# A hybrid decoder block on one core: dilated values formed for two slots at a time

## The chip, the cores and the metric

The kernel runs on one core of a Trainium2 chip. The metric is the device time of one execution in microseconds (us); lower is better. The kernel before takes 1284.16 us, the median of three runs (1284.13 to 1284.34).

The engines are called PE (TensorE, matrix products), DVE (VectorE), ACT (ScalarE), POOL (GpSimd) and SP (SyncE, which here only issues transfers). PE reads its operands from on-chip memory and adds its products up in banks of 512 float columns, which DVE and ACT read. Each engine works through its own instructions in the order in which the program wrote them; an instruction that waits for another engine holds up everything behind it on its own engine.

## The reference, cut to what matters

```python
h = h + 0.5 * swiglu(rms_norm(h, g_ffn1), w_ffn1_gate, w_ffn1_up, w_ffn1_down)
u = rms_norm(h, g_mix)
z = u @ w_in
a_glu, q, k, v, gate_logits = jnp.split(z, split_pts, axis=-1)
y_conv = conformer_conv(a_glu, w_dw, b_dw, g_conv_ln, b_conv_ln, w_conv_out)
q, k = rotary(q, cos, sin), rotary(k, cos, sin)
for gi, (window, dilation) in enumerate(((128, 1), (512, 4), (2048, 16))):
    hs = slice(gi * 4, (gi + 1) * 4)
    o_g, lse_g = dilated_window_attention(q[:, :, hs], k[:, :, hs], v[:, :, hs],
                                          dilation, window // dilation)
alpha = softmax(stack(lses), axis=0)
y_attn = sum(alpha * outs) @ w_attn_out
h = h + (sigmoid(g_a) * y_conv + sigmoid(g_b) * y_attn) @ w_mix_out
h = h + 0.5 * swiglu(rms_norm(h, g_ffn2), ...)
h = h + sigmoid(rms_norm(h, g_ple) @ w_ple_gate) * (p @ w_ple_proj)
return rms_norm(h, g_final)
```

512 positions, width 1024, 12 heads of 128 in three groups of four. The four heads of a group are the four "slots": slot s is head s of each group.

## The kernel before, in words

**Operands.** Every float operand is cut into a high and a low part (`split`, L466: ACT casts the high part, DVE subtracts the rest), and every product is three: high times high, high times low, low times high (`mm3`, L453). Weights come in slabs of 128 x 1024 in the order that `slab_order` (L134) lists. `slab(key)` (L436) is called when a slab is used, and at that moment it starts the work on later ones: loads up to `AHEAD + RAW` slabs ahead, sums of weights up to `AHEAD + SUMS` ahead (`sum_one`, L296; L317, L321, L325 and L340 on DVE), and their splits `AHEAD` = 2 slabs ahead (`split_one`, L392; L402 on ACT, L403 on DVE). For slabs of the kinds "win", "v", "v0", "ao" and "co" the low part is formed by a transfer: ACT writes the negated high part (L372), and POOL issues a transfer that adds the weight to it (L374), four slabs ahead. The slab buffers come from a pool of 16.

**A unit** (`unit`, L458) is 24 products of 512 columns, eight blocks of 128 rows times three, summed in one bank. Its argument `beside` maps a block number to a function that is called ahead of that block and so puts other products among the unit's own.

**The loop over slots** (L1371 to L1431) runs four times. Each time it forms, in this order:

- the value of the first group (slab "v0"): one unit, then L1378; it is transposed later by `turn0`, ahead of block 6 of the next unit;
- three times a query and a key: six units, each followed by `rotary` (L1178; L1180, L1181, L1182, L1188, L1190, L1195, then L1200 or L1203);
- the values of the two dilated groups (slab "v", two per slot): for each of 8 blocks of rows, 4 classes of positions and 3 products, one product of 256 columns, into two banks; then four casts (L1424) and four subtractions (L1427).

**Attention** (class at L1216) of a slot is spread over the next slot's units. `last` forms the scores of the dilated groups ahead of blocks 4 and 6 of the next slot's first unit (L1248 reads them); `step(n)` is called after unit n: n = 0 starts `soft`, the exponentials (L1264) and an exchange of statistics through DRAM (SP, L1160 and L1164 into the tile `other`); n = 4 and 5 transpose the weights (`turn`, L1311, L1316, L1317); n = 5 and 6 multiply them with the values (`values`, banks `po`). `fill(n)` is called from `rotary`: n = 2 reads `other` (`weigh(0)`, L1282 to L1285), n = 3 computes the factors and scales the weights (L1287 to L1296). The unit with n = 4 carries the slot's own scores of the first group and starts their exponentials. Functions put on the list `soon` are taken by `some(n)`, two and four at a time in `rotary` and six after the first unit of a slot. Functions on the list `between` run in the next `rotary`.

**Background.** The depthwise convolution is a list `bg` of DVE instructions (31 taps per tile, L1087 and L1094, closed by L1099 and L1112). `background(n)` takes the next n: 4 after the first unit of a slot, 3 in each `rotary`, 1 after each block of the dilated values and 1 more in each half of their evacuation. After the slots come 16 gate units (L1485 to L1502), each with `side(6)`: six items of `bg`, or, once `bg` is empty, one step of `lns`. `lns` (L1469) is the layer norm of the convolution in 19 steps; a gate unit takes one more of them ahead of its block 4 (`half`). Its `root` forms the sums on PE (`ss`), its `spread` the row R, `normal` scales (L1445), `swish` applies silu (L1449) and splits (L471 and L472) two tiles each. Eight half units `ao` (L1506) take one step each; what is left runs ahead of the `co` units.

**The `co` units and the mixing.** Eight units `co` (L1521) multiply the normed convolution (`cvh`, `cvl`) with their weights. After each, up to `N_FORM` = 10 jobs of the list `later` run, then L1527 and L1528 form the gated sum, then new jobs are listed by `form_pair` (L630; L639 and L654 on DVE, L651 on ACT). After the last unit `N_FIRST` = 7 jobs run. Then the mixing product (L1540) goes through seven quarter products in the order B11, T1, T2, B22, T3, B21, T4 (`quarters_of`, L702); B11 and T2 share the bank `pa`, and after each one `add` (L713; L726) adds the bank to the residual `h`.

Of the kernel before, what the change touches and what calls it, by code (L numbers as in the profile page):

```python
# [10 lines left out]
F32 = mybir.dt.float32  # L11
# [7 lines left out]
P = 128  # L19
# [56 lines left out]
        ("dn", 2, 0), ("dn", 2, 1), ("gu", 9), ("gu", 10), ("dp", 0), ("dn", 3, 0), ("dn", 3, 1))  # L76
BY_ = False
N_FORM = 10
N_FIRST = 7
AFTER_M = {"B11": 0, "T1": 3, "T2": 3, "B22": 2, "T3": 2, "B21": 2, "T4": 2}  # L80
AFTER = {"B11": 1, "B21": 1, "T2": 1, "T1": 1, "T3": 2, "B22": 2}
# [52 lines left out]
def slab_order():  # L134
    out = []
    out += ffn_order("1")
    for c in range(KD):
        out += [("win", 8 + c), ("win", c)]
    for s in range(NSLOT):
        out += [("v0", s)]  # L140
        for g in range(NG):
            out += [("win", 16 + 4 * g + s), ("win", 28 + 4 * g + s)]
        out += [("v", s, j) for j in range(2)]
    out += [("win", 48 + m) for m in range(KD)]
    out += [("win", 40 + m) for m in range(KD)]
    out += [("ao", j) for j in range(4)]
    out += [("co", m) for m in range(KD)]
    out += [("m", ("mx", g), q) for g in range(2) for q in MIXED]
    out += ffn_order("2")
    out += [("pT",), ("pp", 0), ("pp", 1)]  # L150
    out += [("pg", m) for m in range(KD)]
    return out
# [3 lines left out]
def block_kernel(ctx: ExitStack, tc: tile.TileContext, a, out):  # L156
# [17 lines left out]
    def T(n, dt=F32, w=S):  # L174
        return act.tile([P, w], dt, name=name(n), tag="t", bufs=NT)
# [11 lines left out]
    def by_block(t):  # L187

        return t.rearrange("p (c b i) -> p b c i", c=NB, b=NB)

    def blocks(t):

        return t.rearrange("p (b c i) -> p b c i", c=NB, b=NB)

    def bank(n="ps", tag="ps"):
        return psum.tile([P, S], F32, name=name(n), tag=tag, bufs=6 if tag == "ps" else 2)
# [31 lines left out]
    def sources(key):  # L228

        if key[0] == "v0":  # L230
            return [(slice(2 * j, 2 * j + 2), slice(0, HD), blocks_of(a["w_v"][key[1], j], 2)[:, :, :HD])
                    for j in range(4)]
        if key[0] == "v":
            return [(slice(2 * i, 2 * i + 2), slice(0, 2 * HD), blocks_of(a["w_v"][key[1], 2 * key[2] + i], 2)[:, :, HD:])
                    for i in range(2)]
        if key[0] == "gq":
            return row_of(quarter(key[1], ("gu", key[2]), key[3]))
        if key[0] == "dp":
            at, k = (2 * P * z for z in ROUNDS[key[2]])
            return row_of([a["w_ffn%s_down" % key[1]][key[3] + i][:, at:at + k] for i in range(2)])  # L240
        src = source(key)
        if len(src.shape) == 3:
            return [(slice(0, KD), slice(0, P), src)]
        return [(None, slice(0, src.shape[-1]), src)]

    def blocks_of(t, k):
        return t.rearrange("p (k c) -> p k c", k=k)
# [11 lines left out]
    def product(key):  # L259
        return key[2] if key[0] in ("1", "2", "m") else None  # L260
# [162 lines left out]
    def ahead(what, one, to):  # L423
        while state[what] < min(to, len(order)):
            one()
# [10 lines left out]
    def slab(key):  # L436
        i = state["use"]
        assert order[i] == key, (order[i], key)
        state["use"] = i + 1
        more, sums = (1, 1) if key[0] == "gq" else (MORE, SUMS)  # L440
        for j in range(i + 1, i + AHEAD + sums + 1):
            ahead("load", load_one, j + 1)
            ahead("sum", sum_one, j + 1)
            soon_(i, j)
            ahead("split", split_one, min(j, i + AHEAD) + 1)
        if state["early"] < len(order) and product(order[state["early"]]) == "T4":
            soon_(i, i + LEAD["T4"])
        ahead("load", load_one, i + AHEAD + RAW + 1)
        if product(order[min(i + AHEAD + RAW, len(order) - 1)]):
            ahead("load", load_one, i + AHEAD + RAW + more + 1)  # L450
        return halves.pop(i)

    def mm3(ps, wh, wl, xh, xl, start, stop, part=False):  # L453
# [4 lines left out]
    def unit(ps, key, xs, ks=range(KD), beside={}):  # L458
        h, l = slab(key)
        for k in ks:  # L460
            if k in beside:
                beside[k]()
            c = slice(k * P, (k + 1) * P)
            mm3(ps, h[:, c], l[:, c], xs[k][0], xs[k][1], k == ks[0], k == ks[-1])

# [902 lines left out]

            return {2: (nothing, lambda: self.weigh(0)), 3: (scale, nothing)}.get(n, (nothing,) * 2)

    before = None  # L1371
    for s in range(NSLOT):
        q, k = [], []
        now = Attention(q, k)
        p = bank("pq")
        unit(p, ("v0", s), us, beside=before.last() if before else {})
        v0 = T("v0")
        V.tensor_mul(blocks(v0), by_block(p), by_block(R))  # L1378
        p = None
        if before is not None:  # L1380
            before.step(0)
        some(6)
        background(N_V0)

        def turn0():
            p = bank("pt")
            for b in range(NB):
                PE.transpose(p[:, b * P:(b + 1) * P], v0[:, b * P:(b + 1) * P], ident)
            now.v0 = split(p, "v")

        n = 1
        for g in range(NG):
            for base, dst in ((16, q), (28, k)):
                p = bank("pq")
                unit(p, ("win", base + 4 * g + s), us,
                     beside=now.scores(range(NB)) if n == 4 else {N_TURN: turn0} if n == 1 else {})
                if before is not None:
                    before.step(n)
                if n == 4:
                    now.soft(range(NB))  # L1400
                dst.append(rotary(p, "qk", N_QK[n - 1], g == 0, g > 0 and base == 16, *([before.fill(n)] if before else [])))
                p = None
                n += 1
        v0 = None
        q = k = None
        pv = [bank("pv") for _ in range(2)]
        for j in range(2):
            wh, wl = (blocks_of(z, 4) for z in slab(("v", s, j)))
            for kk in range(4):
                for c in range(NB):  # L1410
                    xh, xl = (classes(z)[:, c] for z in us[4 * j + kk])
                    po, at = pv[c // 2][:, c % 2 * 2 * P:(c % 2 + 1) * 2 * P], 4 * j + kk
                    PE.matmul(po, xh, wh[:, kk], start=at == 0 and c % 2 == 0, stop=False, skip_group_check=True)
                    PE.matmul(po, xh, wl[:, kk], start=False, stop=False, skip_group_check=True)
                    PE.matmul(po, xl, wh[:, kk], start=False, stop=at == KD - 1, skip_group_check=True)
                background(N_V)
        wh = wl = None
        now.v = []
        for c in range(NB):
            now.v.append(T("v12", F32R))  # L1420
        zs = [pv[c // 2][:, c % 2 * 2 * P:(c % 2 + 1) * 2 * P] for c in range(NB)]
        for cs in ((0, 2), (1, 3)):
            for c in cs:
                A.activation(now.v[c][:, :2 * P], zs[c], AF.Copy, scale=rcls[:, c:c + 1])  # L1424
            background(1)
            for c in cs:
                V.scalar_tensor_tensor(now.v[c][:, 2 * P:], zs[c], rcls[:, c:c + 1], now.v[c][:, :2 * P].bitcast(F32),  # L1427
                                       op0=OP.mult, op1=OP.subtract)
        now.v = [(t[:, :2 * P], t[:, 2 * P:]) for t in now.v]
        pv = zs = None  # L1430
        before, now = now, None  # L1431


# [52 lines left out]
    for base in (48, 40):  # L1486
        for m in range(KD):
            p = bank("pg")
            unit(p, ("win", base + m), us, beside={4: half} if n else before.last())
            t = T("sg")  # L1490
            V.tensor_mul(t, p, R)
            A.activation(t, t, AF.Sigmoid)
            sg[base, m] = t
            if n < 10:
                before.step(n, 2)
                some(6)
                for f in before.fill(n - 1):
                    f()
                while between:
                    between.pop(0)()  # L1500
            n += 1
            side(N_GATE)  # L1502
    before = None
    us.clear()
    background(len(bg))
    for j in range(4):  # L1506
# [14 lines left out]
    for m in range(KD):  # L1521
        p = bank("py")
        unit(p, ("co", m), cv)
        for _ in range(min(N_FORM, len(later))):
            next_job(later)
        t = sg[40, m]
        V.tensor_mul(t, t, p)  # L1527
        V.tensor_add(t, t, sg.pop((48, m)))  # L1528
        if m < 4:
            begun.append(form_pair(t, None, mixes[m], by=BY))  # L1530
        else:
            form_pair(sg.pop((40, m - 4)), sg.pop((40, m)), mixes[m - 4], None, begun[m - 4], BY)
# [205 lines left out]
```

## Time and profile before

| | us |
|---|---|
| median of three runs | 1284.16 |
| the profiled execution, its own time | 1284.48 |
| its span in the profile | 1282.6 |
| slots 0 to 3 (first "v0" unit to the last value product) | about 437 to 666.5 |
| gate units | 666.5 to 764.0 |
| `ao`, `co`, start of the mixing | 764.0, 786.3, 829.8 |

A row of a timeline gives the start of an instruction from the start of the span, its duration, engine, line, operation, what it writes and reads, and in brackets the engine's idle time before it and what ended it. A merged row (x4) gives the whole stretch. A row of windows gives the stretch, then for each engine asked for its busy time and count, then the granted clock, the share of the transfer engines and GB/s. A row of waits names who waited for whom: total, times, longest. Matmul durations overlap; what counts is the time from one start to the next.

### The profile page before, as it was taken

Reading aid. Unit: us, or ns where it says so; the run is one execution under the profiler, and the core shown is the slowest. Engines: PE = TensorE matmul, PEld = TensorE weight load, DVE = VectorE, ACT = ScalarE, POOL = GpSimd, SP = SyncE. Lnnn points to the kernel's source line nnn. Section 1 sums busy time; section 2 is a strip of 40 time slices with the busy share of each in tenths; the row PEclk is TensorE's granted clock in tenths of the full one; section 3 lists DMA queues with packets and bytes.
Section 4 is the critical chain, followed back from the end, with each engine's and each line's share of the span. In section 5 each row is a group of like instructions: output and inputs, shape, how many; then the busy total and the mean of one; then the engine's idle time right before and its main releaser. Section 6 shows DMA issues by size and latency. Waiting matters only on the chain.

```text
span 1282.6 us, 21795 instructions
## 1 busy us (share of the span) xinstructions
PE 1268.7 (99%) x8266; PEld 1163.1 (91%) x8266; DVE 1015.2 (79%) x1617; ACT 741.4 (58%) x1088; POOL 300.6 (23%) x392
## 2 busy tenths in 40 slices
PE   9999999999999999999999999999999999999997
PEld 7899999998988888989898888898899999998986
DVE  6988778898969887878778756786988888785865
ACT  6667566575633264746555445363777566585652
POOL 3122132132223232323332222012122122132000
PEclk9999999999999999999999999999999999999999
DMA  9676886867879889897887779567576876868641
GB/s 295 155 171 160 199 208 152 207 166 191 193 180 231 208 154 202 152 191 150 172 184 169 167 186 224 144 134 206 132 188 152 203 205 147 211 157 198 145 106 59
DMA packets 118224, 226.12 MB, mean 176 GB/s; under 512 B 20584, under 2 KB 54760, under 8 KB 118120
## 3 DMA queue, kind: packets, MB, share of 16 engines
q0 software_dynamic: 49600, 142.10, 54.3%
q1 hardware_dynamic: 68232, 82.37, 20.5%
q8 instruction: 65, 1.06, 0.3%
q14 instruction: 39, 0.32, 0.1%
q10 hardware_dynamic: 288, 0.26, 0.1%
HBM read 168.56 MB, written 2.13 MB: 133 GB/s over the span
## 4 chain that ended last, share of the span: by engine, by line
PE 74%; DVE 3%; DMA 1%; issue 1%; ACT 0%; SPq 0%; DVEq 0%
PE pa L708 5%; PE pa L709 5%; PE pa L711 5%; PE pq L454 4%; PE pq L455 4%; PE pq L456 4%; PE pg L454 3%; PE pg L456 3%; PE pg L455 3%; PE pd L711 2%; PE pd L709 2%; PE pd L708 2%; PE pb L455 2%; PE pb L454 2%; PE pb L456 2%; PE pe L711 1%
## 5 line engine op out<-in xcount | busy, mean ns | idle before, releaser
L374 POOL DMA_DIRECT2D wl<-wr x108 | 93.4, 867 | 439.8 <-ACT wl L372 341.1
L708 PE MATMUL pa<-bh,wh 128*128 128x256 f32 x680 | 167.5, 283 | 0.5 <-DVE gx L723 0.4
L709 PE MATMUL pa<-bl,wh 128*128 128x256 f32 x680 | 167.2, 283 | 0.0
L1094 DVE SCALAR_TENSOR_TENSOR acc<-glu,taps,acc 128x511 f32<-128x511 f32 (+14 forms) x240 | 161.6, 733 | 0.0
L403 DVE TENSOR_TENSOR wl<-s,wh 128x1024 fp32r<-128x1024 f32 (+1 forms) x96 | 108.5, 1132 | 38.1 <-ACT wh L402 37.8
L372 ACT ACTIVATE wl<-wh 128x1024 fp32r<-128x1024 f32 x84 | 87.9, 1051 | 80.3 <-DMA wh<-in_w_in 54.8
L708 PEld LDWEIGHTS pa<-bh,wh 128*128 128x128 f32 x680 | 130.5, 192 | 1.0 <-issue 0.5
L709 PEld LDWEIGHTS pa<-bl,wh 128*128 128x128 f32 x680 | 130.5, 192 | 0.0
L372 ACT ACTIVATE wl<-wr 128x1024 fp32r<-128x1024 f32 (+1 forms) x108 | 105.8, 980 | 26.0 <-DVE wl L403 11.5
L402 ACT ACTIVATE wh<-s 128x1024 fp32r<-128x1024 f32 (+1 forms) x96 | 92.9, 969 | 35.0 <-PE pd L455 13.4
L386 ACT ACTIVATE wh<-wr 128x1024 fp32r<-128x1024 f32 (+1 forms) x108 | 105.5, 977 | 12.0 <-PE pd L711 6.1
L708 PE MATMUL pd<-bh,wh 128*128 128x256 f32 x448 | 110.3, 283 | 0.0
L709 PE MATMUL pd<-bl,wh 128*128 128x256 f32 x448 | 110.2, 283 | 0.0
L374 POOL DMA_DIRECT2D wl<-in_w_in x56 | 48.5, 869 | 219.7 <-ACT wl L372 200.6
L711 PE MATMUL pa<-bh,wl 128*128 128x256 f32 x680 | 96.9, 283 | 0.0
L454 PE MATMUL pq<-xsh,wh 128*128 128x512 f32 x224 | 88.7, 396 | 0.0
L711 PEld LDWEIGHTS pa<-bh,wl 128*128 128x128 f32 x680 | 88.4, 192 | 0.0
L455 PE MATMUL pq<-xsl,wh 128*128 128x512 f32 x224 | 87.3, 390 | 0.0
L456 PE MATMUL pq<-xsh,wl 128*128 128x512 f32 x224 | 87.3, 390 | 0.0
L708 PEld LDWEIGHTS pd<-bh,wh 128*128 128x128 f32 x448 | 86.0, 192 | 0.0
L709 PEld LDWEIGHTS pd<-bl,wh 128*128 128x128 f32 x448 | 86.0, 192 | 0.0
L454 PE MATMUL pg<-xsh,wh 128*128 128x512 f32 x192 | 76.2, 397 | 0.3 <-ACT xsh L474 0.3
(330 smaller groups left out, 3615.4 us busy)
## 6 DMA issues: line engine op xcount, KB each, us to landing
wl<-wr POOLq DMA_DIRECT2D x72, 512.0 KB, 5.6
wh<-in_w_in POOLq DMA_DIRECT2D x56, 512.0 KB, 7.2
wl<-in_w_in POOLq DMA_DIRECT2D x56, 512.0 KB, 6.0
wr<-in_w_ffn_up SPq DMA_DIRECT2D x80, 256.0 KB, 4.3
wr<-in_w_ffn_gate SPq DMA_DIRECT2D x78, 256.0 KB, 4.7
wr<-in_w_ffn_down SPq DMA_DIRECT2D x96, 192.0 KB, 3.8
wl<-wr POOLq DMA_DIRECT2D x36, 384.0 KB, 4.4
wr<-in_w_ffn_down SPq DMA_DIRECT2D x16, 256.0 KB, 4.5
```

The lines of the kernel that those rows point to most:

```text
L372: A.activation(l.bitcast(F32R), h, AF.Copy, scale=-1.0)
L374: G.dma_start(to, src, accum_op=OP.add)
L386: A.activation(h, r, AF.Copy)
L402: A.activation(h, r, AF.Copy)
L403: V.tensor_sub(l, r, h.bitcast(F32))
L454: PE.matmul(ps, wh, xh, start=start, stop=False, skip_group_check=part)
L455: PE.matmul(ps, wh, xl, start=False, stop=False, skip_group_check=part)
L456: PE.matmul(ps, wl, xh, start=False, stop=stop, skip_group_check=part)
L708: PE.matmul(o, h[:, c], th, start=q in ("B11", "B21", "T1") and i == 0, stop=False, skip_group_check=True)
L709: PE.matmul(o, h[:, c], tl, start=False, stop=False, skip_group_check=True)
L711: PE.matmul(o, l[:, c], th, start=False, stop=i >= len(at) - 2, skip_group_check=True)
L1094: bg.append(lambda acc=acc, g=g, w=w, s=s: V.scalar_tensor_tensor(acc[:, s:], g[:, :S - s], w, acc[:, s:], op0=OP.mult, op1=OP.add))
```

## The change

The dilated values are formed once for two slots, after the six rotary units of slots 0 and 2: four slabs, each with two blocks of rows of both slots side by side, so that each product has 512 columns; four banks; the usual `split` empties them. In slots 1 and 3 the first group's unit comes last instead of first, and the steps of the slot before are counted one unit earlier. `beside` may hold several functions per block. In the `co` units from the fourth on, `slab` looks three ahead instead of two, and after the last `co` unit only three of the ten jobs run ahead of L1527 and L1528, the other seven after them.

```diff
+N_LAST = 3
...
     for s in range(NSLOT):
-        out += [("v0", s)]
-        for g in range(NG):
-            out += [("win", 16 + 4 * g + s), ("win", 28 + 4 * g + s)]
-        out += [("v", s, j) for j in range(2)]
+        qk = [("win", z + 4 * g + s) for g in range(NG) for z in (16, 28)]
+        out += qk + [("v0", s)] if s % 2 else [("v0", s)] + qk
+        out += [("v", s, j) for j in range(0 if s % 2 else 4)]
...
         if key[0] == "v":
-            return [(slice(2 * i, 2 * i + 2), slice(0, 2 * HD), blocks_of(a["w_v"][key[1], 2 * key[2] + i], 2)[:, :, HD:])
+            return [(slice(i, 4, 2), slice(0, 2 * HD), blocks_of(a["w_v"][key[1] + i, key[2]], 2)[:, :, HD:])
                     for i in range(2)]
...
-        for j in range(i + 1, i + AHEAD + sums + 1):
+        ahead_ = AHEAD + (key[0] == "co" and key[1] >= 3)
+        for j in range(i + 1, i + ahead_ + sums + 1):
...
+    def values_of(s):
+
+        pv = [bank("pv") for _ in range(NB)]
+        for j in range(4):
+            wh, wl = (blocks_of(z, 2) for z in slab(("v", s, j)))
+            for c in range(NB):
+                for kk in range(2):
+                    at = 2 * j + kk
+                    xh, xl = (classes(z)[:, c] for z in us[at])
+                    PE.matmul(pv[c], xh, wh[:, kk], start=at == 0, stop=False)
+                    PE.matmul(pv[c], xh, wl[:, kk], start=False, stop=False)
+                    PE.matmul(pv[c], xl, wh[:, kk], start=False, stop=at == KD - 1)
+                if c % 2:
+                    background(2 * N_V)
+        vs = [split(pv[c], "v", rcls[:, c:c + 1]) for c in range(NB)]
+        background(2)
+        return vs
...
+        odd, turned0 = s % 2, {}
+
+        def first_group(n):
+
+            p, v0 = bank("pq"), T("v0")
+            unit(p, ("v0", s), us, beside=joined(before.last() if before and not odd else {}, pending))
+            pending.clear()
+            V.tensor_mul(blocks(v0), by_block(p), by_block(R))
+            p = None
+            if before is not None:
+                before.step(n)
+            some(6)
+            background(N_V0)
...
+            pending[N_TURN] = turn0
+
+        if not odd:
+            first_group(0)
         n = 1
         for g in range(NG):
             for base, dst in ((16, q), (28, k)):
                 p = bank("pq")
-                unit(p, ("win", base + 4 * g + s), us,
-                     beside=now.scores(range(NB)) if n == 4 else {N_TURN: turn0} if n == 1 else {})
+                beside = before.last() if n == 1 and odd else now.scores(range(NB)) if n == 4 else {}
+                unit(p, ("win", base + 4 * g + s), us, beside=joined(beside, pending))
+                pending.clear()
                 if before is not None:
-                    before.step(n)
+                    before.step(n - odd)
...
-                dst.append(rotary(p, "qk", N_QK[n - 1], g == 0, g > 0 and base == 16, *([before.fill(n)] if before else [])))
+                dst.append(rotary(p, "qk", N_QK[n - 1], g == 0, g > 0 and base == 16,
+                                  *([before.fill(n - odd)] if before else [])))
...
+        if odd:
+            first_group(6)
...
+        if s % 2 == 0:
+            values = values_of(s)
+        now.v = [(h_[:, s % 2 * 2 * P:][:, :2 * P], l_[:, s % 2 * 2 * P:][:, :2 * P]) for h_, l_ in values]
         before, now = now, None
...
-        for _ in range(min(N_FORM, len(later))):
+        for _ in range(min(N_FORM if m < KD - 1 else N_LAST, len(later))):
             next_job(later)
         t = sg[40, m]
         V.tensor_mul(t, t, p)
         V.tensor_add(t, t, sg.pop((48, m)))
+        if m == KD - 1:
+            for _ in range(min(N_FORM - N_LAST, len(later))):
+                next_job(later)
```

The old value loop (L1406 to L1430) is gone. The first gate unit carries what slot 3 left pending (`turn0`).

More of the change, by code (lines that the diff above doesn't have):

```diff
@@ L444, in slab @@
             soon_(i, j)
-            ahead("split", split_one, min(j, i + AHEAD) + 1)
+            ahead("split", split_one, min(j, i + ahead_) + 1)
         if state["early"] < len(order) and product(order[state["early"]]) == "T4":
             soon_(i, i + LEAD["T4"])
-        ahead("load", load_one, i + AHEAD + RAW + 1)
-        if product(order[min(i + AHEAD + RAW, len(order) - 1)]):
-            ahead("load", load_one, i + AHEAD + RAW + more + 1)
+        ahead("load", load_one, i + ahead_ + RAW + 1)
+        if product(order[min(i + ahead_ + RAW, len(order) - 1)]):
+            ahead("load", load_one, i + ahead_ + RAW + more + 1)
         return halves.pop(i)
@@ L461, in unit @@
             if k in beside:
-                beside[k]()
+                for f in beside[k] if isinstance(beside[k], list) else (beside[k],):
+                    f()
             c = slice(k * P, (k + 1) * P)
@@ L1369, in fill, with joined @@
             return {2: (nothing, lambda: self.weigh(0)), 3: (scale, nothing)}.get(n, (nothing,) * 2)
-    before = None
+    def values_of(s):
[14 more added lines that the diff above has]
+        return vs
+    def joined(x_, y):
+        return {k: [f for z in (x_, y) if k in z for f in [z[k]]] for k in {**x_, **y}}
+    before, pending = None, {}
     for s in range(NSLOT):
@@ L1374, in block_kernel, with turn0 @@
         now = Attention(q, k)
[L1375 to L1389, printed above, removed]
+        odd, turned0 = s % 2, {}
[9 more added lines that the diff above has]
+            background(N_V0)
+            def turn0(now=now):
+                p = bank("pt")
+                for b in range(NB):
+                    PE.transpose(p[:, b * P:(b + 1) * P], v0[:, b * P:(b + 1) * P], ident)
+                now.v0 = split(p, "v")
+            pending[N_TURN] = turn0
+        if not odd:
+            first_group(0)
         n = 1
@@ L1399, in block_kernel @@
                 if n == 4:
                     now.soft(range(NB))
-                dst.append(rotary(p, "qk", N_QK[n - 1], g == 0, g > 0 and base == 16, *([before.fill(n)] if before else [])))
+                dst.append(rotary(p, "qk", N_QK[n - 1], g == 0, g > 0 and base == 16,
+                                  *([before.fill(n - odd)] if before else [])))
                 p = None
                 n += 1
-        v0 = None
+        if odd:
+            first_group(6)
+        beside = None
@@ L1405, in block_kernel @@
         q = k = None
[L1406 to L1428, printed above, removed]
@@ L1429, in block_kernel @@
-        now.v = [(t[:, :2 * P], t[:, 2 * P:]) for t in now.v]
-        pv = zs = None
+        if s % 2 == 0:
+            values = values_of(s)
+        now.v = [(h_[:, s % 2 * 2 * P:][:, :2 * P], l_[:, s % 2 * 2 * P:][:, :2 * P]) for h_, l_ in values]
         before, now = now, None
@@ L1488, in block_kernel @@
             p = bank("pg")
-            unit(p, ("win", base + m), us, beside={4: half} if n else before.last())
+            unit(p, ("win", base + m), us, beside={4: half} if n else joined(before.last(), pending))
             t = T("sg")
@@ L1502, in block_kernel @@
             side(N_GATE)
-    before = None
+    before = values = None
     us.clear()
```

## The prediction

> **What bounds the kernel now.** I read the page first (engines, clock, chain), then who PE waited for, then the stages that the diff touches, in windows and timelines. From the page:
>
> ```profile
> PE 1268.7 (99%) x8266; PEld 1163.1 (91%) x8266; DVE 1015.2 (79%) x1617; ACT 741.4 (58%) x1088; POOL 300.6 (23%) x392
> ...
> PEclk9999999999999999999999999999999999999999
> ...
> PE 74%; DVE 3%; DMA 1%; issue 1%; ACT 0%; SPq 0%; DVEq 0%
> ```
>
> PE is busy 99% of the span at the full granted clock, and the chain that ended last runs over PE. So an edit pays in two ways only: PE streams less, or one of its few waits goes; and it costs as soon as PE meets a wait that it does not have today. Among PE's own waits one of size lies in a part that the diff touches:
>
> ```profile
> PE pa L708 <- ACT wh L402: 1.3, 1, 1.3
> ```
>
> **Part 1, the products of the dilated values.** Before, 96 products of 256 columns per slot; after, 96 products of 512 columns for two slots. Here are windows over one old value stage, over all four together, and over two rotary units (48 products of 512 columns; the counts include one product that reaches in from before):
>
> ```profile
> 477.37:488.88 11.51, 11.51 (x97) 11.51 (x96) 10.46 (x17) 5.40 (x8) 3.65 (x5) 1.00 1.00 199
> ...
> sum 46.01, PE 46.01 PEld 46.01 DVE 40.95 ACT 22.18 POOL 16.92; mean PE 11.50 PEld 11.50 DVE 10.24 ACT 5.55 POOL 4.23
> ```
>
> ```profile
> 449.60:460.48 10.88, 10.88 (x49) 1.00 0.65 136
> ```
>
> A 256-column product takes 11.50/96 = 0.1198 us from start to start, a 512-column one 10.88/48 = 0.2267 us. Four stages cost 46.0 us now and will cost 2 x 96 x 0.2267 = 43.5 us: **2.5 us less on PE**. The 512-column form with a new stationary operand for each product is the one that the rotary units run, so I take its price as it is; the other bound is that two 256-column times remain, a gain of 0. The bytes, DMA count and 1 KB pieces of the slabs stay the same.
>
> The Trainium skill, "TensorE: Matmul & The Clock Gate", section "Back-to-back issue gap", gives an isolated warm gap of N/2.4 + 2.5 ns. By that 192 merged pairs would save 192 x 2.5 ns = 0.5 us (an estimate from that page). The rows above show about 13 ns saved per pair instead; they decide here.
>
> **Part 2, the last unit's sum and the longer look ahead.** DVE and PE rows around the start of the mixing products:
>
> ```profile
> 825.30 0.69 DVE L1528 TENSOR_TENSOR sg<-sg,sg 128x512 f32<-128x512 f32 x1
> 825.91 1.22 DVE L403 TENSOR_TENSOR wl<-s,wh 128x1024 fp32r<-128x1024 f32 x1
> 827.04 1.22 DVE L325 TENSOR_TENSOR wr<-wr,wr 128x1024 f32<-128x1024 f32 x1
> 828.18 0.42 DVE L639 TENSOR_TENSOR t<-sg,t 128x256 f32<-128x256 f32 x1
> ...
> 831.18 0.68 DVE L1527 TENSOR_TENSOR sg<-sg,py 128x512 f32<-128x512 f32 x1
> ...
> 834.96 1.22 DVE L403 TENSOR_TENSOR wl<-s,wh 128x1024 fp32r<-128x1024 f32 x1
> 836.10 0.75 DVE L726 SCALAR_TENSOR_TENSOR h<-pa,h 128x256 f32<-128x256 f32 x2
> ```
>
> ```profile
> 834.57 1.12 PE L711 MATMUL pd<-b,wl 128*128 128x256 f32 x8
> 836.99 0.36 PE L708 MATMUL pa<-b,wh 128*128 128x256 f32 x1 [1.30 <-ACT wh L402]
> ```
>
> The wait view names ACT, but T2 accumulates in the bank from which L726 reads B11, and L726 ends at 836.85, just before PE goes on. DVE is the late one. The stall is 836.99 - 835.53 = 1.46 us (eight products of 0.12 from 834.57 end the slot at 835.53).
>
> The look ahead moves each weight sum and split one unit forward, so the 1.13 us of T2's L403 (834.96 to 836.10) leaves the stretch before L726. But with only three jobs ahead of L1527, and only one of them on DVE (L639), DVE comes to L1527 early: L403 of T1 and L325 go to unit 6, so unit 7 starts about 1.1 us later (L1528 ends at 827.1), then L403 of T2 to 828.3 and L639 to 828.6. PE ends unit 7 at 829.8 (835.53 less the 48 products of B11 and T1), and L1527 can read its sum at about 829.95. DVE idles 1.3 us before it, time that it used for jobs until now. From there follow 3.78 us (831.18 to 834.96: L1527, L1528 and the seven jobs of `N_FIRST`) and 2.66 us (the seven jobs left over: 3.00 from 828.18 to 831.18 less 0.34 for L639), less some 0.4 of waits for ACT that the longer row of jobs covers: L726 at 836.0, done at 836.75, T2 at 836.85. **I take 0.15 us gained**; bounds 1.46 gained (stall gone) and 0.3 lost.
>
> **Part 3, what the order of slots moves.** Two places, both off PE today.
>
> *The layer norm of the convolution.* The old value stage takes 8 + 2 items per slot from the `background` queue, 40 in all; the new one takes 4 x 4 + 2 = 18 per pair, 36 in all. Four taps move to the gate units. Today the queue ends exactly with the sixth item after unit 9 (three taps, two casts, one sum in these rows), after 10 x 6 = 60 items. With 64 it ends one unit later, and since `lns` starts only when it is empty, each of its steps comes two steps, one whole unit, later.
>
> ```profile
> 729.95 1.97 DVE L1094 SCALAR_TENSOR_TENSOR acc<-glu,taps,acc 128x483 f32<-128x483 f32 x3
> 731.96 1.49 DVE L1112 TENSOR_TENSOR csum<-csum,cv 128x512 f32<-128x512 f32 x2
> ...
> 772.86 0.69 DVE L1514 TENSOR_TENSOR sg<-sg,pb 128x512 f32<-128x512 f32 x1 [2.53 <-PE pb L456]
> 773.47 2.48 DVE L1445 TENSOR_TENSOR cv<-cv,R 128x512 f32<-128x512 f32 x4
> ...
> 787.19 0.69 DVE L472 TENSOR_TENSOR cvl<-cv,cvh 128x512 fp32r<-128x512 f32 x1 [0.68 <-ACT cvh L471]
> ```
>
> ```profile
> 774.18 0.82 ACT L1449 ACTIVATE cv<-cv,gx 128x512 f32<-128x512 f32 x1 [3.65 <-DVE cv L1445]
> ...
> 776.94 1.04 ACT L372 ACTIVATE wl<-wh 128x1024 fp32r<-128x1024 f32 x1
> ...
> 783.37 1.05 ACT L372 ACTIVATE wl<-wh 128x1024 fp32r<-128x1024 f32 x1
> 784.32 0.80 ACT L1449 ACTIVATE cv<-cv,gx 128x512 f32<-128x512 f32 x1
> 785.16 0.63 ACT L471 ACTIVATE cvh<-cv 128x512 fp32r<-128x512 f32 x1
> 785.69 0.80 ACT L1449 ACTIVATE cv<-cv,gx 128x512 f32<-128x512 f32 x1
> ```
>
> ```profile
> 786.26 0.39 PE L454 MATMUL py<-cvh,wh 128*128 128x512 f32 x1
> ...
> 791.25 0.39 PE L455 MATMUL py<-cvl,wh 128*128 128x512 f32 x1
> ```
>
> The last low half is ready at 787.88 and wanted at 791.25: 3.37 us to spare. The chain (ACT does one tile in 785.69 - 784.32 = 1.37 us) would start 5.44 us later, two `ao` products of 24 x 0.2267 together; one L372 (0.95 us of pitch) falls ahead of it rather than in it. Ready at 787.88 + 5.44 - 0.95 = 792.37, against 791.25: **1.1 us of new stall in the first `co` unit, 1.2 with restarts**. Bounds: 0 (other work gives way) and 2.1 (the L372 stays inside).
>
> *The odd slots.* There the old v0 unit no longer stands ahead of the first rotary unit, so `step(0)` comes in a rotary unit, whose ACT work goes first, and `fill` sits beside `soft`.
>
> ```profile
> 497.27 0.69 DVE L1378 TENSOR_TENSOR v<-pq,R 128x512 f32<-128x512 f32 x1 [0.64 <-PE pq L456]
> ...
> 508.62 0.69 DVE L1180 TENSOR_TENSOR rot<-pq,nl 128x512 f32<-128x512 f32 x1 [0.67 <-DMA wh<-in_w_v]
> ...
> 511.91 0.16 DVE L1282 TENSOR_TENSOR jm<-own,other 128x8 f32<-128x8 f32 x1
> ...
> 514.05 0.69 DVE L1180 TENSOR_TENSOR rot<-pq,nl 128x512 f32<-128x512 f32 x1 [0.48 <-PE pq L456]
> ```
>
> ```profile
> 498.08 0.51 ACT L1264 ACTIVATE sc<-sc,nm 128x256 f32<-128x256 f32 x1 [3.62 <-DVE nm L1259]
> ...
> 512.02 0.63 ACT L1195 ACTIVATE qkh<-rot 128x512 fp32r<-128x512 f32 x1 [1.48 <-DVE rot L1190]
> ...
> 516.06 1.60 ACT L1296 ACTIVATE sc<-sc,jm 128x128 f32<-128x128 f32 x4
> ```
>
> ```profile
> 503.30 2.57 SPq L1164 DMA_DIRECT2D other<-st  x4
> ```
>
> ```profile
> other<-st SPq DMA_DIRECT2D x16, 1.0 KB, 5.6
> ```
>
> ```profile
> 520.75 0.93 PE L1311 MATMUL pt<-ident,sc 128*128 128x128 f32 x7
> ```
>
> The unit's products end at about 497.1. Four exponentials run 498.08 to about 500.1 (3.0 us after), then the statistics travel: the last `other` issue starts at about 505.3 and lands 5.6 us later, 510.9; L1282 needs them at 511.91, 1.0 us to spare. In an odd slot the exponentials split around L1195, which starts 3.4 us after L1180 (508.62 to 512.02): the last ends 0.2 + 3.4 + 0.6 + 1.0 = 5.2 us after the unit, 2.2 later. DVE would wait at L1282 for 2.2 - 1.0 + 0.35 (the transposes of v0 are no longer in that stretch) = 1.6 us, and reaches L1180 of unit 4 about 1.5 us late. Then ACT has two exponentials (1.0 us) ahead of the four scalings: first scaling 2.0 + 1.0 us after L1180, fourth done 1.6 us later, so 0.2 + 1.5 + 4.6 = 6.3 us after the end of unit 4. PE wants them for L1311 5.44 us after it, and the last of them some 0.4 later. Stall 0.5 us in each of two slots, **1.0 us in all**; bounds 0 and 1.7 each (a late landing). Today these tiles wait 3.1 us (scaled at 516.06 + 1.60 = 517.66, read at 520.75).
>
> The new evacuation, four casts (0.63 us each by the L471 row) and four subtractions of 512 columns per stage, lies behind the next unit's products, which write other banks: nothing, and about 3 us per stage if that cover were gone. The held `po` banks, the two first-group units in a row and the four value slabs in a row find other free banks and a weight lead of four slabs (22 us), so nothing.
>
> **The sum**, against the profiled execution's own 1284.48: -2.5 - 0.15 + 1.2 + 1.0 = -0.45 us, 1284.0; the median of the three runs is 0.32 lower, so **1283.7**.
>
> **Rivals.**
>
> *All covered.* ACT and DVE keep more slack than my rows give (DVE is 79% busy), and neither new wait reaches PE: -2.65, 1281.5. With the T2 stall gone as well: -2.5 - 1.46, 1280.2. For it: today's margins of 1 to 3 us are all positive. Against: the count of 64 items is arithmetic, not timing.
>
> *The odd slots decide.* One mechanism: the statistics land later than 5.6 us after issue, DVE stands at L1282, the scalings are late, and PE stands at L1311 in both slots. This row of the tile `other` shows that DVE did wait once today:
>
> ```profile
>   DMA other<-st: 1.6, 1
> ```
>
> A landing x us later costs 2x: slower by 0.2% (2.57 us) needs -0.45 + 2x > 2.57, x above 1.5 us. With x = 2, 1287.7.
>
> *Wider products gain nothing.* If columns alone set the time, 512 columns cost twice 0.1198 us: the 2.5 us goes, 1286.2. The 512-column row speaks against. The Trainium skill's page on TensorE, named above, would put the truth near this end.
>
> *The sum is not read ahead in effect.* That is in my forecast: DVE gets there early and waits for PE.
>
> **How the numbers follow.** A measurement here tells 0.2%, 2.57 us, from no change. Forecast 0.55 (its own range 1282.4 to 1285.4); all covered 0.16 at 1281.5 and 0.10 at 1280.2; odd slots 0.13; no gain of wide products 0.03; something unnamed 0.03. Faster than 1281.6: 0.10, half of the 0.16, and the forecast's lower tail, 0.24. Slower than 1286.7: 0.14. The rest 0.62. The range 1280.9 to 1286.3 leaves out a tenth on each side.
>
> **What would show it.** Two value stages of 21.8 us each, 192 products at 0.2267; T2's first product again behind L726, with DVE idle before the last L1527; PE waiting for `cvl` in the first `co` unit; DVE waiting for `other` twice in odd slots, PE waiting for L1296 at L1311. No such waits would give 1281.5; PE waiting for a DMA of `w_v`, or a bank, would make the whole forecast wrong.

## The result and the profile after

The changed kernel takes 1286.35 us (median of 21 runs, 1285.08 to 1287.4), the kernel before, in the same comparison, 1284.32 (21 runs). The ratio is 1.0015, with a 95% interval of 1.0009 to 1.0020: 2.0 us slower, where 0.45 us faster was forecast. The profiled execution shows the same step: a span of 1284.6 us against 1282.6. Lines of the changed kernel are two higher up to the loop over slots (L1282 is now L1284, L1311 is L1313) and 12 higher behind it (L1527 is L1539).

The page of the changed kernel, engines and chain, and then the view of PE's waits (total, times, longest):

```profile
PE 1268.3 (99%) x8074; PEld 1153.6 (90%) x8074; DVE 1011.4 (79%) x1609; ACT 738.2 (57%) x1080; POOL 300.0 (23%) x392
...
PE 72%; DVE 3%; ACT 2%; DMA 1%; issue 1%; SPq 0%; DVEq 0%
```

```profile
PE pt L1313 <- ACT sc L1298: 1.8, 2, 1.6
PE pa L710 <- DVE h L728: 1.1, 1, 1.1
...
PE py L456 <- DVE cvl L474: 0.5, 2, 0.2
```

PE has 192 products fewer, yet its busy time falls by only 0.4 us: the ends of matmuls are modelled, and part of a wait counts as busy (the `co` units below are 1.35 us longer than before at 0.9 us more busy time). The waits show what is new: one at the weight transposes, and one for `cvl`. How long the stages take is seen in windows (stretch, its length, busy time of PE and so on, then the granted clock). Here are the two value stages; the same stretch of slot 1 and of slot 3, from the end of the scores to the start of the last products with the values; and the `co` units:

```profile
477.46:499.22 21.76, 21.76 (x98) 18.03 (x96) 14.95 (x23) 5.95 (x7) 7.88 (x10) 1.00 1.05 222
597.46:619.24 21.78, 21.78 (x97) 18.04 (x97) 17.16 (x30) 8.99 (x13) 8.87 (x12) 1.00 1.05 233
...
523.77:547.51 23.74, 21.87 (x108) 17.55 (x107) 16.06 (x39) 18.68 (x39) 5.93 (x8) 1.00 0.77 153
643.80:664.59 20.79, 20.79 (x108) 17.64 (x107) 16.32 (x38) 15.93 (x35) 5.97 (x8) 1.00 0.75 168
...
786.63:831.50 44.87, 44.41 (x193) 35.90 (x192) 30.77 (x52) 20.39 (x32) 5.39 (x7) 1.00 0.72 184
```

The value stages take 43.54 us where four took 46.07 (-2.53). The `co` units take 44.87 instead of 43.52 (+1.35). Slot 1 needs 23.74 us for the same products for which slot 3 needs 20.79 (+2.95). The wait of T2 is the fourth place:

```profile
831.71 0.69 DVE L1539 TENSOR_TENSOR sg<-sg,py 128x512 f32<-128x512 f32 x1 [1.38 <-PE py L457]
...
837.65 0.75 DVE L728 SCALAR_TENSOR_TENSOR h<-pa,h 128x256 f32<-128x256 f32 x2
```

```profile
836.30 1.12 PE L713 MATMUL pd<-b,wl 128*128 128x256 f32 x8
838.54 0.36 PE L710 MATMUL pa<-b,wh 128*128 128x256 f32 x1 [1.12 <-DVE h L728]
```

The eight products from 836.30 end the slot at 837.26, so T2 stalls 1.28 us (1.46 before: -0.18); DVE idles 1.38 us ahead of L1539. The four add up to -2.53 + 1.35 + 2.95 - 0.18 = +1.59; the other 0.4 lies in stretches with the same work in both kernels (from T2's first product to the end of the span: 446.0 against 445.6 us).

Slot 1 is the largest. The DVE rows of slot 1, then the same rows of slot 3, in which PE does not stall:

```profile
521.15 0.69 DVE L1192 TENSOR_TENSOR rot<-rot,sw 128x512 f32<-128x512 f32 x1
526.36 0.17 DVE L1284 TENSOR_TENSOR jm<-own,other 128x8 f32<-128x8 f32 x1 [4.52 <-DMA other<-st]
...
527.35 0.28 DVE L1250 CUSTOM_DVE_ANT_0 sc<-sc,mask 128x128 f32<-128x128 f32 x1
...
528.79 0.69 DVE L1182 TENSOR_TENSOR rot<-pq,nl 128x512 f32<-128x512 f32 x1
...
641.17 0.69 DVE L1192 TENSOR_TENSOR rot<-rot,sw 128x512 f32<-128x512 f32 x1
642.73 0.17 DVE L1284 TENSOR_TENSOR jm<-own,other 128x8 f32<-128x8 f32 x1 [0.86 <-DMA other<-st]
...
645.39 0.69 DVE L1182 TENSOR_TENSOR rot<-pq,nl 128x512 f32<-128x512 f32 x1
```

SP's issues in both slots (first three rows slot 1), and the view of transfers over slot 1, then over slot 3 (size, us from issue to landing):

```profile
512.63 0.39 SPq L1162 DMA_DIRECT2D st<-own  x1
517.98 1.76 SPq L1166 DMA_DIRECT2D other<-st  x4
519.97 0.79 SPq L271 DMA_DIRECT2D wr<-in_w_v  x1
...
632.66 0.38 SPq L1162 DMA_DIRECT2D st<-own  x1
635.74 2.39 SPq L1166 DMA_DIRECT2D other<-st  x4
```

```profile
st<-own SPq DMA_DIRECT2D x1, 4.0 KB, 5.3
...
st<-own SPq DMA_DIRECT2D x1, 4.0 KB, 3.1
```

The exchange starts 11.14 us ahead of the end of the scores in both slots (523.77 - 512.63 and 643.80 - 632.66). In slot 1 its first transfer takes 5.3 us instead of 3.1, and the second starts when the first has landed. DVE gets `other` 4.52 us late instead of 0.86. In slot 1 L1182 is 3.4 us later than in slot 3, measured from the end of the scores, and the scalings L1298 are 3.7 us later.

It looks as if DVE's wait reached PE by way of L1182. But a second thing hangs on the exchange. SP's third row loads the raw first-group weight of slot 2 (`wr<-in_w_v`, in four parts), and SP comes to it only when the exchange is issued. In the new order the first-group units of slots 1 and 2 stand one behind the other, so ACT wants this weight soon. ACT's rows:

```profile
527.80 1.06 ACT L372 ACTIVATE wl<-wr 128x1024 fp32r<-128x1024 f32 x1 [0.18 <-DMA wr<-in_w_v]
528.77 1.04 ACT L386 ACTIVATE wh<-wr 128x1024 fp32r<-128x1024 f32 x1
529.82 0.59 ACT L1183 ACTIVATE sw<-pq 64x512 f32<-64x512 f32 x1
...
531.93 1.59 ACT L1298 ACTIVATE sc<-sc,jm 128x128 f32<-128x128 f32 x4
```

L372 and L386, which make the two parts of that weight, stand ahead of L1183 and the scalings on ACT. Which of the two waits counts is seen in last10, an experiment below with the same slot 1. There `other` came 1.44 us earlier (first DVE, then ACT rows):

```profile
524.92 0.17 DVE L1284 TENSOR_TENSOR jm<-own,other 128x8 f32<-128x8 f32 x1 [3.11 <-DMA other<-st]
...
527.35 0.69 DVE L1182 TENSOR_TENSOR rot<-pq,nl 128x512 f32<-128x512 f32 x1
```

```profile
527.79 1.06 ACT L372 ACTIVATE wl<-wr 128x1024 fp32r<-128x1024 f32 x1 [1.62 <-DMA wr<-in_w_v]
...
529.82 0.59 ACT L1183 ACTIVATE sw<-pq 64x512 f32<-64x512 f32 x1
```

L1182 is 1.44 us earlier too, yet L1183 starts at 529.82 and PE's transposes at 532.37, as in the changed kernel. In all seven profiles that have the exponentials in their new place the first transpose follows the start of L372 by 4.57 or 4.58 us, whereas from L1284 to it there are 6.0 to 7.6 us. So the last link to PE is the weight behind the exchange, through ACT; the wait for `other` lies beside it.

### The profile page after: what moved, and what is told of

The parts are those of the page before. It is cut to its first block, busy times and chain, and to the rows that moved or that the text cites. A ratio compares the mean times of both kernels' runs of the same rounds, so it can differ in the third digit from the quotient of the medians.

```text
span 1284.6 us, 21430 instructions
## 1 busy us (share of the span) xinstructions
PE 1268.3 (99%) x8074; PEld 1153.6 (90%) x8074; DVE 1011.4 (79%) x1609; ACT 738.2 (57%) x1080; POOL 300.0 (23%) x392
## 4 chain that ended last, share of the span: by engine, by line
PE 72%; DVE 3%; ACT 2%; DMA 1%; issue 1%; SPq 0%; DVEq 0%
PE pa L710 5%; PE pa L711 5%; PE pa L713 5%; PE pq L455 3%; PE pq L457 3%; PE pq L456 3%; PE pg L455 3%; PE pg L457 3%; PE pg L456 3%; PE pd L711 3%; PE pd L713 3%; PE pd L710 2%; PE pb L456 2%; PE pb L455 1%; PE pb L457 1%; PE pe L711 1%
## 5 line engine op out<-in xcount | busy, mean ns | idle before, releaser
L372 ACT ACTIVATE wl<-wh 128x1024 fp32r<-128x1024 f32 x84 | 87.9, 1052 | 104.8 <-DMA wh<-in_w_in 73.2
L372 ACT ACTIVATE wl<-wr 128x1024 fp32r<-128x1024 f32 (+1 forms) x108 | 105.7, 979 | 24.6 <-DVE wl L403 12.3
L386 ACT ACTIVATE wh<-wr 128x1024 fp32r<-128x1024 f32 (+1 forms) x108 | 105.4, 976 | 13.8 <-DMA wl<-wr 6.9
```

The costliest lines, as they stand in the source:

```text
L372: A.activation(l.bitcast(F32R), h, AF.Copy, scale=-1.0)
L386: A.activation(h, r, AF.Copy)
```

## The experiments

All are timed against the kernel before, on the same chip and in alternation with it, but for the last two, which were timed once each.

**taps40**: four items instead of two behind the values' evacuation, 40 in all.

```diff
         vs = [split(pv[c], "v", rcls[:, c:c + 1]) for c in range(NB)]
-        background(2)
+        background(4)
```

> Changed kernel with 20 instead of 18 queue items per pair of slots, so that the gate units find 60 items again as in the kernel before. Theory (the sixty-first item puts the layer norm of the convolution a unit later): the statistics products pm stand at about 740 us again instead of 745, the eight co units take 43.5 us instead of 44.87, and the time is 1.35 us below the changed kernel, 0.7 above the kernel before. Rival (ACT's own load ahead of the first co unit is late, whatever the queue): co units stay near 44.8, no change in time. Slots are as in the changed kernel, so the profile is a second look at slot 1: if the late exchange there is the rule, PE waits about 3 us at the weight transposes of slot 1 again and little in slot 3; if it was chance, the two stalls come out anywhere from 0 to 3.

1285.89 us, before 1284.24, ratio 1.0010 (1.0001 to 1.0019). The `co` units in its profile:

```profile
787.60:831.12 43.52, 43.52 (x194) 36.04 (x192) 27.99 (x48) 15.88 (x26) 5.36 (x7) 1.00 0.75 192
```

The wait for `cvl` is gone to the last hundredth, and `pm` stands at 740.8: the count of items was the cause. The median shows only a part of it. The same profile has 24.72 us in slot 1 instead of 23.74, which is taken up below.

**last10**: ten jobs ahead of the last sum, look ahead kept.

```diff
-N_LAST = 3
+N_LAST = 10
```

> Changed kernel with ten jobs again ahead of the last gated sum, the longer look ahead kept. Theory (with only three jobs DVE idles before the last sum's product is there, and then stands behind jobs before it reads B11): DVE has no idle time before the last sum, T2's first product waits about 0.3 us instead of 1.28, and the time is 1.0 us below the changed kernel, 1.0 above the kernel before. Rival (the wait of T2 is set by the jobs between the sum and the reading of B11, or by ACT, not by the idle time): T2 still waits 1.2 us or more and the time does not move. Slots as in the changed kernel: third look at slot 1.

1286.04 us, ratio 1.0015 (1.0006 to 1.0024): no gain that the runs can tell. The last sum, the reading of B11 and T2 in its profile:

```profile
833.43 0.69 DVE L656 TENSOR_TENSOR bl<-t,bh 128x512 fp32r<-128x512 f32 x1 [0.36 <-ACT bh L653]
834.04 0.68 DVE L1539 TENSOR_TENSOR sg<-sg,py 128x512 f32<-128x512 f32 x1
...
837.82 0.75 DVE L728 SCALAR_TENSOR_TENSOR h<-pa,h 128x256 f32<-128x256 f32 x2
```

```profile
837.44 1.12 PE L713 MATMUL pd<-b,wl 128*128 128x256 f32 x8
838.71 0.36 PE L710 MATMUL pa<-b,wh 128*128 128x256 f32 x1 [0.15 <-DVE h L728]
```

The idle time ahead of L1539 is gone and T2 stalls 838.71 - 838.40 = 0.31 us instead of 1.28: the mechanism is as expected. Its profile has 24.88 us in slot 1.

**exp_first**: in odd slots the exponentials and the start of the exchange ahead of the first rotary.

```diff
                     before.step(n - odd)
+                    if odd and n == 1:
+                        some(6)
```

> Changed kernel, but in odd slots the four exponentials and the start of the exchange come right behind step 0, ahead of the first rotary. Theory (the exchange starts 2.2 us or more too late in odd slots, and its landing sets PE's wait at the weight transposes): the first exchange transfer starts about 3 us earlier after the end of the unit, DVE waits at most 1 us for other, PE waits under 0.4 us at the transposes in both odd slots, and the time is 2.9 us below the changed kernel, 0.9 below the kernel before. Rival (the transfers land late in slot 1 because of what else moves then, so an earlier start does not bring an earlier landing): PE still waits 1.5 us or more in slot 1, and the time falls by less than 1.5. Second rival: the rotary behind the exponentials becomes late and PE waits at the scores of the first group instead.

1283.56 us, before 1284.24, ratio 0.9998 (0.9989 to 1.0007), 2.8 below the changed kernel's 1286.35. The exchange starts earlier and the weight behind it with it (issued at 516.23 instead of 519.97), so this edit does not tell the two apart. L1284 has no wait left, and ACT has done L386 at 526.23. But slot 1 still takes 21.85 us, 1.06 too many. DVE's rows show a second wait behind the first, which the late exchange had covered; beside them POOL's issue and that transfer's time to landing:

```profile
522.34 0.16 DVE L1284 TENSOR_TENSOR jm<-own,other 128x8 f32<-128x8 f32 x1
...
526.41 0.29 DVE L1250 CUSTOM_DVE_ANT_0 sc<-sc,mask 128x128 f32<-128x128 f32 x1 [3.00 <-PE pq L457]
```

```profile
519.11 0.85 POOL L374 DMA_DIRECT2D wl<-wr  x1 [3.83 <-ACT wl L372]
```

```profile
wl<-wr POOLq DMA_DIRECT2D x1, 512.0 KB, 7.0
```

The view names PE, but the scores that L1250 reads ended at 522.3. What ended just before it is a transfer: 519.11 + 7.0 = 526.1, the low part of the first group's weight. In odd slots that weight is now prepared in the middle of the slot, and `sc` comes from the same pool of 16 buffers as the weights.

**all_three**: these three edits together.

> The three edits together (20 queue items, ten jobs, exponentials first in odd slots). If the three waits are independent: 1.35 + 1.0 + 2.9 = 5.2 us below the changed kernel, about 3.2 below the kernel before (1281.1). If they overlap or a new wait comes in, less: at worst what the best single one gives.

1281.39 us, ratio 0.9977 (0.9968 to 0.9985): 2.85 below the kernel before. L1250 waits again until a `wl<-wr` has landed, and slot 1 takes 21.88 us.

A second set of runs has the changed kernel again (**after_again**), the first two edits (**two_waits**), the three with the buffer claimed early (**claimed**) and the three alone (**three_again**). What claimed adds:

```diff
         odd, turned0 = s % 2, {}
+        if odd:
+            V.memset(now.sc[0][:, 0:1], 0.0)
```

> The changed kernel unaltered, as the reference on this chip and as a fourth look at slot 1. If the late exchange in slot 1 is the rule, its first transfer lands 5 us after issue again (three profiles: 4.7 to 5.3; 3.1 in slot 3), PE waits 2.5 to 3.2 us at the weight transposes of slot 1 and not at all in slot 3. About 2.0 us above the kernel before.

> Changed kernel with 20 queue items and ten jobs, odd slots as they are: what is left is the merged products (-2.5) and the wait of slot 1 (+2.9), and T2's rest (1.46 to 0.31, -1.15). If the waits add up as PE's rows say: 2.3 us below the changed kernel on this chip, about 0.5 below the kernel before. Rival (the two waits were cover for one another or for something later, since the single edits moved the median by only 0.3 and 0.5): less than 1.2 us below the changed kernel.

> The three edits together, and in odd slots a one-column write claims the buffer of the tile sc before the slot's first unit (its column is read by nothing). In slot 1 of the three-edit version the first masking of scores (L1250) stood 2.6 us until the transfer wl<-wr of the first group's weight had landed (26.1 minus 19.1, a buffer of the weights that sc takes over), and PE then waited 1.05 us at the transposes. Theory (the buffer's earlier owner is that slab's raw weight): claimed early, L1250 runs right behind the scores, PE's wait in slot 1 falls under 0.3 us, and the time is 0.8 to 1.0 us below the three-edit version, 3.7 to 3.9 below the kernel before. Rival (a buffer less for the slabs delays a weight): a new wait of PE on a weight, or on DVE at the claiming write, and no gain. Second rival (the wait of L1250 has another cause): it stays.

> The three-edit version again, on the chip of the other runs of this call, to set the claimed version and the two-wait version against it: 4.9 us below the changed kernel, 2.9 below the kernel before, as in its first run.

| | median, us | before, us | ratio (95%) | slot 1 stretch, us |
|---|---|---|---|---|
| after_again | 1286.49 | 1284.59 | 1.0015 (1.0006 to 1.0024) | 24.58 |
| two_waits | 1283.85 | 1284.59 | 0.9993 (0.9984 to 1.0002) | 23.35 |
| three_again | 1281.31 | 1284.59 | 0.9974 (0.9964 to 0.9984) | 21.51 |
| claimed | 1280.50 | 1284.59 | 0.9967 (0.9954 to 0.9979) | 20.87 |

The two edits, which singly moved little, bring 2.64 together (2.3 expected), so their waits add up. Claimed shows slot 1 without a stall:

```profile
523.35 0.16 DVE L1284 TENSOR_TENSOR jm<-own,other 128x8 f32<-128x8 f32 x1
...
524.33 0.28 DVE L1250 CUSTOM_DVE_ANT_0 sc<-sc,mask 128x128 f32<-128x128 f32 x1
```

```profile
523.44:544.31 20.87, 20.87 (x107) 17.61 (x106) 14.86 (x37) 18.89 (x39) 5.91 (x8) 1.00 0.84 164
```

L1250 follows at once, PE's loss in slot 1 is 0.08 us, and no weight came late there. So the buffer was the cause of the second wait. Against three_again claimed is 0.8 lower, as its stretch says (0.64), but their intervals overlap. It is the fastest version found, 4.1 us below the kernel before.

**claim_only** (the changed kernel and the claim alone) and **mix_undone** (ten jobs, and `ahead_ = AHEAD` everywhere) were timed once each:

> The changed kernel with only the early claim of the buffer of sc in odd slots; the exponentials stay where the change put them. Theory (two waits stand side by side on DVE in slot 1, for other and for the buffer, and the later one counts, which is other, landing at 524.8 to 526.4 against 524.5 for the buffer): L1250 no longer waits by itself, DVE still waits 3 us or more for other, and PE loses 2.2 to 3.2 us at the transposes of slot 1 as before. Rival (the buffer was the larger part): PE's loss there falls under 1.2 us.

> The changed kernel with ten jobs ahead of the last gated sum and the look ahead of two in all co units, that is without its part on the mixing. Theory (the longer look ahead takes T2's low half, 1.13 us, out of the stretch before B11 is read): without it T2's first product waits 1.4 to 1.5 us again as in the kernel before, against 0.31 with the look ahead and ten jobs, and 1.28 with the look ahead and three. Rival (the ten jobs alone do it, the look ahead is without effect): about 0.3.

```profile
524.80 0.17 DVE L1284 TENSOR_TENSOR jm<-own,other 128x8 f32<-128x8 f32 x1 [2.91 <-DMA other<-st]
...
525.79 0.29 DVE L1250 CUSTOM_DVE_ANT_0 sc<-sc,mask 128x128 f32<-128x128 f32 x1
```

With the claim alone DVE still stands 2.91 us at `other`, and slot 1 takes 24.70 us: the buffer is not what holds PE up in the changed kernel. Nor does this tell that `other` is, for here too ACT waits for the raw weight, L372 starts at 527.63 and the first transpose comes 4.58 us later. The time was 1287.04, that of mix_undone 1286.44, beside 1283.7 before. In mix_undone T2's first product:

```profile
836.58 1.12 PE L713 MATMUL pd<-b,wl 128*128 128x256 f32 x8
839.00 0.36 PE L710 MATMUL pa<-b,wh 128*128 128x256 f32 x1 [1.30 <-ACT wh L402]
```

It stalls 839.00 - 837.54 = 1.46 us, as in the kernel before. So the longer look ahead is worth 1.15 us with ten jobs, and the cut to three jobs gave 0.97 of it back.

## Why the prediction was wrong

*The products*: right. -2.5 forecast, -2.53 measured, 21.76/96 = 0.2267 us each. By the Trainium skill, "TensorE: Matmul & The Clock Gate", section "Back-to-back issue gap", it would have been 0.5 us (an estimate from its formula); the trace bears out the rows.

*The mixing*: right, mechanism and size: DVE idle for 1.38 us (1.3 forecast), -0.18 us (-0.15).

*The layer norm*: right. 44.87 - 43.52 = +1.35 us against +1.2, and taps40 removes it by the count alone.

*The odd slots*: here the forecast failed, in the term "1.0 us in all", 0.5 in each of two slots. It measured 2.95 in slot 1 and 0 in slot 3 in the profiled execution. The start of the exchange was right: 5.2 us after the unit. Three things in its working were not, and the third decided:

- The landing was taken from slot 1 of the kernel before, where the first transfer takes 3.1 us. The same profile has 4.8, 4.9 and 4.2 us in the other three exchanges, which the working did not look at. In the changed kernel it takes 4.8 to 5.4 us in slot 1 in all seven profiles with the exponentials in their new place, and 2.9 to 4.3 in slot 3.
- A wait of DVE at L1284 was passed on to L1180 nearly in full, and from there to PE. Slot 3 shows that there is slack: 0.86 us of waiting cost PE nothing, and in after_again and claim_only 1.56 and 1.62 us, as much as the forecast 1.6, cost nothing either (20.78 and 20.79 us for the stretch).
- Of the two first-group units in a row the prediction says that they find "a weight lead of four slabs (22 us), so nothing". But SP issues the raw weight of the second behind the exchange. In the kernel before it had landed at 511.9, and L372 took it up at 527.74. In the changed kernel it landed at 527.56 and L372 started at 527.80, with L1183 and the scalings behind it. This wait, put at nothing, set PE's stall in all seven profiles. The sign named for it, a wait for a DMA of `w_v`, came on ACT and not on PE.

The same sentence says when weights arrive, and not which buffers they hold meanwhile: L1250's wait for one of them was not in the prediction. In the changed kernel it lies under the other waits and costs nothing more; it decides as soon as the exchange is early, 0.7 to 1.1 us in exp_first, all_three and three_again.

The rival "the odd slots decide" had the late landing right, and `other` came some 2.9 us later than assumed where 2.95 us were lost. That the two agree is in part luck, since PE's stall follows the weight and not `other`; and the rival counted both slots where it was one.

So of the 2.65 us between 1283.7 and 1286.35, 1.95 come from slot 1 and 0.15 from the layer norm. The rest is the 0.32 that the forecast took off for the profiled execution and about 0.3 in stretches with the same work in both kernels, less some 0.05 in the other two terms. Two things stay open. Why the first transfer lands later in slot 1 than in slot 3 is not known: both start at the same place of the slot, and no run varied what else moves then. And no run loads that weight ahead of the exchange, so what late statistics would cost by themselves is not measured. As an estimate, L1183 starts 0.72 us behind L1182 in slot 3, where ACT is free; by that it could have started at 529.5 in the changed kernel and at 528.1 in last10, instead of 529.82 in both. So in the first the statistics alone would have cost most of the stall, in the second hardly any.

## What to carry to other kernels

When a chain of work through small transfers is moved, price every leg of it by the slowest of its kind in the trace, look at what the same engine issues behind it and who wants that, and look for the slack of each engine between the wait and the consumer before passing the wait on. When the order of loads changes, ask for each tile of the same pool which buffer it will take over and when that one comes free; a one-column write ahead of time can claim another. And where several waits stand side by side, single undoings show little: undo them together before calling any of them harmless.

## What the runs showed of the hardware

PE's stall in slot 1 has a second price, which the seven profiles with it show in four cases and not in three. In last10 the last product ahead of the transposes starts at 530.35 and the first transpose at 532.37, 1.79 us later than without a stall; windows from there on:

```profile
532.37:534.40 2.03, 1.96 (x10) 1.28 (x11) 1.06 (x3) 2.03 (x6) 0.00 (x0) 1.00 0.86 147
534.41:537.82 3.41, 3.41 (x10) 2.63 (x9) 1.89 (x4) 3.39 (x9) 1.16 (x2) 0.50 0.37 107
537.83:540.93 3.10, 3.10 (x16) 2.53 (x14) 3.06 (x6) 1.79 (x5) 0.26 (x1) 1.00 0.54 41
```

For 3.41 us the granted clock is 0.50, after the stall and while PE is busy. In taps40, after_again and claim_only it lasts 3.41 us too. The 24 products behind the transposes then take 6.65 to 7.17 us instead of 5.58, 1.1 to 1.6 us more. That is in the slot 1 stretches of 24.58 to 24.88 us. Which of the timed executions had it can't be seen from their times, but their mean granted clocks say something. Of the seven profiled executions the four with the stretch have 0.996 or 0.997, the three without it 0.998. Of taps40's eleven executions eight have 0.996 (median 1285.94) and two 0.998 (1283.78 and 1285.46); of the changed kernel's 21, six have 0.996 (1286.72) and ten 0.998 (1286.28). So its share differs from run to run, which would blur what single edits show in a median. That isn't shown, for each profile also ends with a stretch at 0.50, of 3.8 to 7.1 us, which moves the mean too. The stalls ahead of it were no longer than those without it: 1.55 to 1.89 us with, 1.77 to 1.88 without; T2's 1.27 to 1.46 us did it in no profile.

The Trainium skill, "TensorE: Matmul & The Clock Gate", section "What's actually happening", says that the clock falls to half after at least one idle window of 3.4 us, and that windows run freely. The length of 3.41 us and the chance in it agree. That a whole window must be idle does not: here it came behind stalls of 1.55 to 1.89 us with the sparse transposes behind them. No profile without a stall of that length in slot 1 has it there; that the two together set it off is argued, not tested.
